# A two-layer hybrid backbone: filters from stacked fp32r features with mirrored slots side by side, and short convolutions made tile by tile with adding DMAs to DRAM

## The chip, the cores and the metric

The kernel runs on one core of one Trainium2 chip. The core has five engines with instruction streams of their own: TensorE (PE; its weight loads are listed as PEld), VectorE (DVE), ScalarE (ACT), GpSimd (POOL) and SyncE (SP), which here only issues DMAs. Sixteen DMA engines move data between DRAM, SBUF (128 partitions) and, through the compute engines, PSUM (8 banks per partition, where PE writes). The metric is device time in microseconds of one execution, the median of the runs.

## The reference

All is fp32 in and out: 2048 tokens of 1024 channels, 256 context tokens, two layers and a final norm. Layer 0 is a pooling mixer beside grouped-query attention (6 query heads, 2 key heads, 128 wide, 2304 keys). Layer 1 is a Hyena operator of order 2 on 768 channels beside a 2-D Fourier mixing on 256. What the change touches is in layer 1:

```python
def short_conv3(u, w, b):
    up = jnp.pad(u, ((0, 0), (1, 1), (0, 0)))
    return up[:, :-2] * w[0] + up[:, 1:-1] * w[1] + up[:, 2:] * w[2] + b

def hyena_filters(L, w1, b1, w2, b2, w3, freq):
    ...
    hdn = jnp.sin(fr * (hdn @ w2 + b2))
    h = (hdn @ w3).reshape(L, HY_ORDER, 2, HY_WIDTH)
    h = h * decay[:, None, None, :]
    h = h / (jnp.sum(jnp.abs(h), axis=(0, 2), keepdims=True) + EPS)
    zero = jnp.zeros((1, HY_ORDER, HY_WIDTH), f32)
    return jnp.concatenate([h[:, :, 0], zero, h[:0:-1, :, 1]], axis=0)

def hyena_mixer(u, ...):
    uc = short_conv3(u, conv_w, conv_b)
    v, x1, x2 = jnp.split(uc, HY_ORDER + 1, axis=-1)
    k = hyena_filters(L, w1, b1, w2, b2, w3, freq)
    z = v
    for o, gate_o in enumerate((x1, x2)):
        z = gate_o * (fft_long_conv(z, k[:, o]) + skip[o] * z)
    return z
```

So each of 3 x 768 channels gets a convolution with three taps over the tokens, and each of 768 channels two long convolutions with a filter of both directions, made from a small network of 64 hidden features.

## The kernel before

**Numbers.** Where accuracy needs it and speed allows it, a product is split: each operand into a high part of type fp32r and a low part, and three fp32r products are summed (`mm3`, L305, lines 306 to 308 of the profile). Small transforms run as plain fp32 products.

**Tokens.** Token 16 * n1 + n2 stands in slot n2 (16 of them, 128 tokens each), so that a row of 2048 tokens of one group of 128 channels is a tile of 128 channels x 16 slots x 128. The token before is the slot before, at the same n1; only for slots 0 and 15 it is slot 15 or 0, shifted by one n1.

**Stages, in order of time.** (1) Modulation, the filters' network (`hd2`, its hidden features, stored to DRAM in `hdd` in the order in which the groups will want them), layer 0's input projections. (2) Attention, by pairs of blocks of 128 queries. The order of its pieces is written out by hand in the strings of `BLOCK`: S scores, M and E the softmax, T transposes, V values, p a step of weight preparation (`weights`, L1371; ACT, POOL and SP), F or f a step of `filters` (L1116). (3) Layer 0's output projection, layer 1's norm, and layer 1's first four groups of columns (`FIRST`, `project0` at L1635); POOL meanwhile splits 25 tiles of weights, all of which stand ahead in its stream (L1733 to L1738). (4) The other 24 groups of columns, four at a time (`MGROUPS`, L482) over four blocks of 512 tokens, in 192 steps of 12 products (L1994), side by side with the long convolutions. (5) Fourier mixing and the first pass of the output projection. (6) Its last pass and the final norm.

**The order from stage 3 on** is made at build time by a planner (`Jobs`, L345). It keeps a clock; `pe(us)` lets it run on with each piece of PE's work; lanes (`Lane`) hand out the pieces of other work when the clock is within 2.5 us of their planned start; `at` puts a piece at a time; `store` queues a store on SP for the next step. An `Event` holds a lane until the planner has set its time. Each engine then runs its own stream in that order, and waits only for data and buffers.

**The filters (`filters`).** There are 12 units (6 groups of channels, 2 orders) of 8 groups of slots, in 18 steps each. A group takes slots a0 = 2 grp + 1 and a0 + 1 of the forward filter and their mirrored slots 16 - n of the backward one: it makes four products of the hidden features (64 x 128) with `w3` (L1173), multiplies by the decay (`ht`, L1174), makes a negated copy of the backward half (`hn`, L1175), sums absolute values for the norm (L1178, L1181), and adds the 128-point factor of the transform by eight products with the table `dft` (L1200, L1201), forward slot and mirrored slot into one sum. ACT copies to `Xs`, two halves of 64 channels (L1203). After the eighth group POOL runs the 16-point transforms (`fft16`) of the two halves, 6 operations per step, and SP stores the spectrum to `spec`.

**The short convolutions (`conv`, L1818).** In stages 3 and 4 `keep_cols` (L1517) copies a block's columns out of PSUM and stores them, as they are, to `ud` in DRAM. Each of 17 rows of channels is then read back whole (`cu`), and convolved in SBUF: ACT makes the middle term with the bias (`co`, L1829), the first tap in two halves (`tap`, L1834) and the last tap in place (L1842); five adding DMAs, issued from POOL, add the taps to `co`, shifted by a slot (L1837 to L1845). One row follows the other, with planned pauses `CV0` to `CV3` between the steps. The first row of all is convolved by ACT and DVE in `first_unit` (L1659).

**The long convolutions.** `s1` (L1853) turns a unit and makes the first factor, `conv_units` (L1944) runs both 16-point transforms and the product with the filter's spectrum on DVE, `s4` (L1885) makes the last factor on PE and gates with a short-convolved row on DVE. 12 units follow each other on DVE.

Of the kernel before, what the change touches and what calls it, by code (L numbers as in the profile page):

```python
# [20 lines left out]
P = 128  # L21
# [18 lines left out]
EARLY, LATE = (0, 1, 2, 6, 7), (3, 4, 5)  # L40

# [16 lines left out]
def constants():  # L58
    """Tables that depend on the shapes alone."""
# [30 lines left out]
    sel = [[2 * q + 1, (2 * q + 2) % 16, 15 - 2 * q, 14 - 2 * q] for q in range(8)]  # L90
    out["decay"] = np.stack([dec[:, :, q, :] for q in sel], 1)
# [36 lines left out]
def fft16(v, X, T, inv, s=None):  # L128
# [27 lines left out]
    def stt(out, in0, scalar, op, in1):  # L156
        """in0 already has its factor where s does the products, but for the sign"""
        if s is None and len(out.shape) > 3:
            for x in range(out.shape[1]):
                stt(out[:, x], in0[:, x], scalar, op, in1[:, x])  # L160
        elif s is None:
            put(out, lambda: v.scalar_tensor_tensor(out=out, in0=in0, scalar=scalar, in1=in1, op0=ALU.mult, op1=op))
        elif scalar > 0:
            tt(out, in0, op, in1)
        else:
            tt(out, in1, ALU.subtract, in0)
# [4 lines left out]
    tt(at(T, 0, *two), at(X, 0, *two), add, at(X, 2 * e, *two))  # L171
    tt(at(T, 2 * e, *two), at(X, 0, *two), sub, at(X, 2 * e, *two))
# [13 lines left out]
    def tan(n, *dims):  # L186
        """the slots from n on, times the tangent"""
# [16 lines left out]
    # the second four: slots k * e + b * o for b; 11 and 14 have the other sign  # L204
# [35 lines left out]
def tile_net(ctx, tc, i, k, out, keep=None):  # L240
# [9 lines left out]
    def mv(dst, src, eng=None):  # L250
        """a DMA of float32 words, of either type"""
# [22 lines left out]
    def y1_part(kk):  # L274
        """the place of gated channels of layer 1"""
# [6 lines left out]
    hdd = dram("hdd", (8, 64, 4, P))  # L282
# [30 lines left out]
    class Lane:  # L313
        """pieces for one engine, each of so many us, the next one at least so many later, or after an event"""
# [30 lines left out]
    class Jobs:  # L345
        """the order in which work is given to the engines: matrix products in front, the rest when they are that far"""
# [37 lines left out]
        def until(self, done):  # L384
            """let time pass until done()"""
# [15 lines left out]
    def load_wout(sp, wp, w, kks, dst, gb, wait=4.0, eng=sy, ve=v):  # L401
        """output projection times the gate, in two parts, one tile of rows at a time"""
# [21 lines left out]
    def load_gate(wp, n):  # L424
        """the gate of layer n, the same in every partition"""
# [4 lines left out]
    def rstd_steps(sp, ss, n, tag, scale):  # L430
        """ss [p, n] sums of squares -> 1 / sqrt(ss * scale + eps), with a Newton step after the square root"""
# [13 lines left out]
    def normed_steps(sp, xs):  # L445
        """each slab [p, D] of xs -> each row over its root mean square, in place"""
# [13 lines left out]
    def modulated_steps(sp, pp, xs, gs, sh, emit, lo_eng):  # L460
        """transposed, scaled and shifted, in two parts: emit(m) gives their places"""
# [1910 lines left out]
```

## Time and profile before

| what | us |
|---|---|
| median of 3 runs | 3173.34 |
| lowest and highest run | 3167.35, 3176.21 |
| span of the profiled execution, first to last instruction | 3162.6 |
| median less that span | 10.7 |
| PE busy | 2996.1 |
| DVE busy | 2183.2 |
| ACT busy | 1329.8 |
| POOL busy | 1215.5 |

The record gives one profiled execution, with its span and no separate time beside it; so sums are made against its span, and 10.7 us are added to compare with the median. Busy times overlap: an engine's share says how full it is over the whole span, and what sets the time in a stage has to be read in that stage. In the views, `out<-in` are the program's names, `128x512` partitions by elements, `[x <-ENGINE name]` the idle time of the engine before the instruction and what ended it. A plain fp32 product shows as two matmuls. "DMA share" is the mean busy share of the 16 DMA engines. SPq and POOLq are the streams in which SP and POOL issue DMAs.

### The profile page before, as it was taken

The page shows a single profiled execution, that of the slowest core. Times are in us where ns is not written, and L with a number is a line of the kernel's source. Part 1 is how long each engine was busy: PE and PEld are TensorE (multiplying, and loading weights), DVE is VectorE, ACT ScalarE, POOL GpSimd, SP SyncE. Part 2 cuts the span into 40 slices and gives each one's busy share as a digit, 9 for nine tenths or more (in the row PEclk, how much of TensorE's full clock was granted, in tenths as well). Part 3 has the DMA queues.
Part 4 walks back from the last instruction along what each step waited for, and adds up shares of the span by engine and source line. Part 5 has one row for each costly group of instructions (what it writes and reads, how often), then busy time and mean ns, then how long its engine had stood idle before and what let it go on. Part 6 is the DMA issues. An engine that isn't in the chain of part 4 may idle for free. (4 is left out here: it accounts for less than half of the span.)

```text
span 3162.6 us, 49927 instructions
## 1 busy us (share of the span) xinstructions
PE 2996.1 (95%) x18121; PEld 2589.2 (82%) x18121; DVE 2183.2 (69%) x4124; ACT 1329.8 (42%) x3130; POOL 1215.5 (38%) x1595
## 2 busy tenths in 40 slices
PE   8999999799999999999999999999989999988799
PEld 4888888699999998999898778777878787874587
DVE  4775437477777777777776443377789797978556
ACT  4444545355555555555556332322323232232123
POOL 3122223027888887878886344001010100101110
PEclk9999999899999999999999999999999999999899
DMA  6466345534444445444443777678899989976875
GB/s 223 157 202 202 125 132 162 182 107 127 121 140 132 128 127 169 121 125 133 117 115 117 250 261 256 242 258 283 275 290 288 293 282 314 275 260 167 233 210 176
DMA packets 425393, 614.72 MB, mean 194 GB/s; under 512 B 140278, under 2 KB 278200, under 8 KB 416698
## 3 DMA queue, kind: packets, MB, share of 16 engines
q1 hardware_dynamic: 399994, 528.43, 51.0%
q0 software_dynamic: 25152, 83.10, 11.2%
q8 instruction: 143, 2.34, 0.3%
q14 instruction: 104, 0.85, 0.1%
HBM read 388.60 MB, written 187.18 MB: 182 GB/s over the span
## 5 line engine op out<-in xcount | busy, mean ns | idle before, releaser
L303 DVE TENSOR_TENSOR pl<-pt,ph 128x512 fp32r<-128x512 f32 (+1 forms) x480 | 299.8, 633 | 137.1 <-ACT ph L300 136.1
L151 DVE TENSOR_TENSOR gB<-gB 128x256 f32<-128x256 f32 (+3 forms) x442 | 351.6, 845 | 51.2 <-ACT gB L1879 47.3
L300 ACT CAST ph<-pt 128x512 fp32r<-128x512 f32 (+1 forms) x480 | 253.5, 556 | 244.7 <-PE pt L1317 242.3
L306 PE MATMUL dacc<-dh,dw 128*128 128x512 f32 x768 | 312.2, 407 | 40.2 <-DMA dh<-h1T 39.5
L1306 ACT ACTIVATE pb<-S,mx 128x512 f32<-128x512 f32 (+1 forms) x480 | 309.7, 656 | 82.7 <-DVE mx L1298 59.4
L307 PE MATMUL dacc<-dh,dw 128*128 128x512 f32 x768 | 304.7, 397 | 0.0
L308 PE MATMUL dacc<-dh,dw 128*128 128x512 f32 x768 | 304.6, 397 | 0.0
L1295 DVE TENSOR_REDUCE mx<-S 128x1 f32<-128x512 f32 (+1 forms) x480 | 279.9, 629 | 18.6 <-DMA kh<-kT0h 14.0
L303 POOL TENSOR_TENSOR wl<-raw,wh 128x256 fp32r<-128x256 f32 x160 | 135.6, 880 | 368.6 <-ACT wh L300 356.7
L1317 PE MATMUL pt<-ident,pb 128*128 128x128 f32 x1728 | 248.0, 275 | 11.2 <-ACT pb L1306 10.9
L151 POOL TENSOR_TENSOR fX<-fT 128x128 f32<-128x128 f32 (+2 forms) x336 | 246.7, 757 | 4.9
L1329 PE MATMUL o<-ph,vh 128*128 128x256 f32 x864 | 233.0, 301 | 1.4 <-ACT ph L300 1.2
L151 POOL TENSOR_TENSOR fT<-fX 128x1024 f32<-128x1024 f32 (+1 forms) x192 | 202.6, 1081 | 49.0 <-ACT fX L1203 44.6
L1317 PEld LDWEIGHTS pt<-ident,pb 128*128 128x128 f32 x1728 | 197.2, 141 | 28.2 <-ACT pb L1306 14.8
L1330 PE MATMUL o<-ph,vl 128*128 128x256 f32 x864 | 216.5, 282 | 1.5 <-DMA vl<-vl 1.5
L306 PEld LDWEIGHTS dacc<-dh,dw 128*128 128x128 f32 x768 | 147.9, 193 | 78.2 <-DMA dh<-h1T 46.7
L306 PE MATMUL S<-kh,qh 128*128 128x512 f32 (+1 forms) x480 | 196.9, 410 | 9.9 <-DMA kl<-kT0l 8.2
L306 PE MATMUL acc<-wh,hh 128*128 128x256 f32 x672 | 197.2, 293 | 3.5 <-ACT qraw L969 2.4
L308 PE MATMUL acc<-wh,hl 128*128 128x256 f32 x672 | 193.1, 287 | 1.2 <-DVE hl L303 0.9
L307 PE MATMUL acc<-wl,hh 128*128 128x256 f32 x672 | 192.8, 287 | 0.9 <-POOL wl L303 0.8
L307 PE MATMUL S<-kl,qh 128*128 128x512 f32 (+1 forms) x480 | 180.4, 376 | 1.1 <-DMA kl<-kT0l 1.0
L308 PE MATMUL S<-kh,ql 128*128 128x512 f32 (+1 forms) x480 | 180.4, 376 | 0.0
(473 smaller groups left out, 7776.5 us busy)
## 6 DMA issues: line engine op xcount, KB each, us to landing
dh<-h1T SPq DMA_DIRECT2D x172, 512.0 KB
dec<-cst_decay_dram SPq DMA_DIRECT2D x96, 256.0 KB
spec<-fX SPq DMA_DIRECT2D x24, 1024.0 KB
dw<-wi SPq DMA_DIRECT2D x48, 512.0 KB
gK<-spec SPq DMA_DIRECT2D x48, 512.0 KB
raw<-in_ev_w_in_dram SPq DMA_DIRECT2D x160, 128.0 KB
u<-dev SPq DMA_DIRECT2D x70, 256.0 KB
cu<-u POOLq DMA_DIRECT2D x17, 1024.0 KB, 8.3
```

Source lines behind the costliest of these rows:

```text
L151: put(out, lambda: v.tensor_tensor(out=out, in0=in0, in1=in1, op=op))
L300: s.copy(hi, src)
L303: lo_eng.tensor_sub(lo, src, hi.bitcast(F32))
L306: pe.matmul(acc, ah, bh, start=first, stop=False)
L307: pe.matmul(acc, ah, bl, start=False, stop=False)
L308: pe.matmul(acc, al, bh, start=False, stop=last)
L1295: v.tensor_reduce(out=B["mx"][:, c : c + 1], in_=S[:, :n], axis=AX.X, op=ALU.max)
L1306: s.activation(B["pb"][:, c * 512 : c * 512 + n], B["S"][c][:, :n], AF.Exp, bias=B["mx"][:, 5:6], accum_out=B["sm"][:, c : c + 1])
L1317: pe.transpose(pt[:, t, :], B["pb"][:, (4 * c + t) * P : (4 * c + t + 1) * P], ident)
L1329: pe.matmul(gr["o"], vh[:, a, :], ph[:, t, :], start=a == 0, stop=False)
L1330: pe.matmul(gr["o"], vl[:, a, :], ph[:, t, :], start=False, stop=False)
```

## The change

**Filters.** The hidden features are split into a high and a low part and stacked to 128 rows; `w3` is split in the same way, each part held twice, one for each half of the rows. A group now takes a slot n and its mirror 16 - n (`PAIRS`; the last takes slots 0 and 8), both of the forward and of the backward filter: two slots, each with two products of K = 128, 256 wide, of type fp32r, the second slot's with forward and backward exchanged. The sign of the imaginary part stands in a new table `fdft`, and the transform's first step restores it (`conj`). So `hn` is gone, and the transform's factor takes four products of 256 columns, and in the last group four of 128 of a sum and a difference. The norm's sums are kept for the eight groups and reduced once. One transform of full width replaces two of half width, 4 operations per step instead of 6.

**Short convolutions.** They are made from each block of 512 tokens as it leaves PSUM, before anything is stored: ACT makes the middle term and the whole far tap of the block, DVE adds the other tap within the block and the piece kept from the block before, SP stores the sum to `ud`, and an adding DMA from POOL adds the far tap to `ud` in DRAM, shifted by a slot. The outermost slots of a row are kept (`edges`, `firstd`) and added at its end. `conv` only loads the finished row. The four `far` quarters lie where `cu` was. The three convolved rows of stage 3 are made in the same way in `first_conv`, straight from PSUM.

**Around these.** The last two groups of columns are ordered anew; `udone` is set 5 steps later; `hf` and the final gain take other buffers; `DE_` = 5 buffers for the blocks of columns. The planned delays are CV0 = 0.3, CV_S = 1.7, CV1 = 2.5, CV2 = 6 and CV3 = 10 us (before: CV0 to CV3 = 14, 12, 8, 15). In the diff, the products with `sd` are those of a unit's last group, and `jobs.until(lambda: not edges)` stands after the last step of stage 4.

```diff
-    MGROUPS = [..., (24, 25, 26, 27), (16, 22, 17, 23)]
+    MGROUPS = [..., (16, 22, 24, 25), (17, 23, 26, 27)]
...
+            s.copy(hd1.bitcast(F32R), hd2)
+            v.tensor_sub(hd2.bitcast(F32R), hd2, hd1)
+            for x, part in enumerate((hd1, hd2)):
+                for half in range(2):
+                    sy.dma_start(hdd[x * 64 : x * 64 + 64, 8 * half : 8 * half + 8, :],
+                                 part[half * 64 : half * 64 + 64].rearrange("p (a b) -> p a b", a=8))
...
-                    for q, n in enumerate((a0, a1, N2 - a0, (N2 - a1) % N2)):
-                        pe.matmul(acc[:, q, :], hd[:, q, :], w3[:, q // 2, :], start=True, stop=True)
-                    v.tensor_mul(ht, acc, dec)
-                    v.scalar_tensor_tensor(out=hn, in0=acc[:, 2:4, :], scalar=-1.0, in1=dec[:, 2:4, :], ...)
+                for q in range(2):
+                    for x in range(2):
+                        w = w3[:, x, ::-1] if q else w3[:, x]
+                        pe.matmul(acc[:, q], hd[:, q, :], w, start=x == 0, stop=x == 1)
+                v.tensor_mul(ht, acc, dec.unsqueeze(2).to_broadcast([P, 2, 2, P]))
...
-                            pe.matmul(fa[:, r, q, :], dft[:, n, r, :], ht[:, q, :], start=True, stop=False)
-                            pe.matmul(fa[:, r, q, :], dft[:, b, r, :], hn[:, q, :] if r else ht[:, 2 + q, :], ...)
+                            pe.matmul(fa[:, r, q], dft[:, b, r, :], sd[:, r, q], start=True, stop=True)
+                            pe.matmul(fa[:, r], dft[:, b, r, :], ht[:, q], start=q == 0, stop=q == 1)
+                s.copy(X[:, :, n : m + 1 : m - n, :], fa)
...
+    def short_conv(jobs, ep, mt, u, tb, up):
+        w0, w1, w2, o = taps(mt)
...
+        yield 0.0, CV0
+        mid = ep.tile([P, 4, P], F32, tag="ev", name="dm")
+        s.activation(mid, u, AF.Identity, bias=col2[:, PK2["cb"] + mt : PK2["cb"] + mt + 1], scale=w1)
+        far = nextfar()
+        s.mul(far, u, wf)
+        yield 0.0, CV_S
+        v.scalar_tensor_tensor(out=mid[:, own], in0=u[:, of], scalar=wn, in1=mid[:, own], op0=ALU.mult, op1=ALU.add)
+        if tb == first:
+            edges[mt] = ep.tile([P, P], F32, tag="eb", name="deb", bufs=4)
+        else:
+            v.tensor_add(mid[:, other], mid[:, other], edges[mt])
+        s.mul(edges[mt], u[:, next_], wn)
+        jobs.lanes[0].took(jobs.now, 0.8)
+        def put():
+            sy.dma_start(o[:, n0 : n0 + 4], mid)
...
+        def more():
...
+                add_to(o[:, n0 - 1 + x : n0 + 3], far[:, x:])
...
+        jobs.at(jobs.now + CV1, 0.0, put)
+        jobs.at(jobs.now + CV2, 0.0, more)
...
-            u = per.tile([P, N2, P], F32, tag="u", name="cu")
-            QU.dma_start(u, ud[mt].rearrange("p (a b) -> p a b", a=N2))
...
-            s.activation(o, u, AF.Identity, bias=..., scale=col2[:, 18 + mt : 19 + mt])
...
-                    g.dma_start(o[:, 1:9], t, accum_op=ALU.add)
...
-            g.dma_start(o[:, :15], u[:, 1:], accum_op=ALU.add)
-            g.dma_start(o[:, 15, : P - 1], u[:, 0, 1:], accum_op=ALU.add)
+            QU.dma_start(o, ud[mt].rearrange("p (a b) -> p a b", a=N2))
             yield 0.0, CV3
...
+            jobs.until(lambda: not edges)
```

More of the change, by code (lines that the diff above doesn't have):

```diff
@@ L40 @@
 EARLY, LATE = (0, 1, 2, 6, 7), (3, 4, 5)
+FIRST = (0, 1, 6, 7)
+PAIRS = [(n, N2 - n) for n in range(1, 8)] + [(0, 8)]
 BLOCK = [
@@ L89, in constants @@
     dec = dec.reshape(128, 16, NCH, P).transpose(2, 0, 1, 3)
-    sel = [[2 * q + 1, (2 * q + 2) % 16, 15 - 2 * q, 14 - 2 * q] for q in range(8)]
-    out["decay"] = np.stack([dec[:, :, q, :] for q in sel], 1)
+    out["decay"] = np.stack([dec[:, :, list(q), :] for q in PAIRS], 1)
+    fd = np.stack([dre, dim], 2)
+    fd[:, 9:, 1] *= -1
+    out["fdft"] = fd
     d = np.arange(256, dtype=f64)
@@ L170, in fft16 @@
     two = ((16, 2), (o, 4), (e, 2)) if inv else ((16, 2), (e, 2), (o, 4))
-    tt(at(T, 0, *two), at(X, 0, *two), add, at(X, 2 * e, *two))
-    tt(at(T, 2 * e, *two), at(X, 0, *two), sub, at(X, 2 * e, *two))
+    if conj:
+        for r, plus, minus in ((0, add, sub), (16, sub, add)):
+            for to, op in ((0, plus), (8, minus)):
+                tt(at(T, r + to, (1, 8)), at(X, r, (1, 8)), op, at(X, r + 8, (1, 8)))
+    else:
+        tt(at(T, 0, *two), at(X, 0, *two), add, at(X, 2 * e, *two))
+        tt(at(T, 2 * e, *two), at(X, 0, *two), sub, at(X, 2 * e, *two))
     row = (o, 4)
@@ L281, in tile_net @@
     wevd, wod = ([dram(f"w{x}{kk}", (P, 2, D)) for kk in range(KD)] for x in "eo")
-    hdd = dram("hdd", (8, 64, 4, P))
+    firstd = [dram(f"first{mt}", (P, P)) for mt in range(18)]
+    hdd = dram("hdd", (P, N2, P))
     fnd = dram("fn", (P, 2, 2, 256))
@@ L1654, in project0, with first_conv, rest, edge @@
                 jobs.pe(0.65 * len(ns))
+        before = {}
+        def first_conv(n, mt, u, tb):
+            w0, w1, w2, o = taps(mt)
+            n0 = 4 * tb
+            mid = ep.tile([P, 4, P], F32, tag="ev", name="cm")
+            s.activation(mid, u, AF.Identity, bias=col2[:, PK2["cb"] + mt : PK2["cb"] + mt + 1], scale=w1)
+            low = ep.tile([P, P], F32, tag="cl", name="cl", bufs=3)
+            s.mul(low, u[:, 0], w2)
+            def rest():
+                for to, of, w in ((slice(1, 4), slice(0, 3), w0), (slice(0, 3), slice(1, 4), w2)):
+                    v.scalar_tensor_tensor(out=mid[:, to], in0=u[:, of], scalar=w, in1=mid[:, to], op0=ALU.mult, op1=ALU.add)
+                if tb:
+                    v.tensor_add(mid[:, 0], mid[:, 0], before[n])
+                else:
+                    before[n] = ep.tile([P, P], F32, tag=f"cb{n}", name="cb", bufs=1)
+                s.mul(before[n], u[:, 3], w0)
+                dve.took(jobs.now, 1.4)
+                jobs.store(o[:, n0 : n0 + 4], mid)
+                if tb == 0:
+                    jobs.store(firstd[mt], low)
+                jobs.at(jobs.now + 4.0, 0.0, edge)
+            def edge():
+                if tb:
+                    add_to(o[:, n0 - 1], low)
+                if tb == NB - 1:
+                    add_to(o[:, 0, 1:], before[n][:, : P - 1])
+                    add_to(o[:, 15, : P - 1], firstd[mt][:, 1:])
+            jobs.at(jobs.now + 1.3, 0.0, rest)
         columns = [Event() for _ in range(NB)]
@@ L1991, in tile_net @@
         with ExitStack() as ps:
-            ep = pool(ps, "d_e", DE)
+            ep = pool(ps, "d_e", DE_)
+            u8 = per.tile([P, N2, P], F32, tag="u", name="far")
+            convlane.append(jobs.lane())
+            fars.extend(u8[:, 4 * x : 4 * x + 4] for x in range(4))
             pm = pool(ps, "d_ps", 1, PSUM)
```

202 lines of the change are left out of this document (106 added, 96 removed).

## The prediction

> **What bounds the kernel now.** I first read the windows view with the span cut at the kernel's stages: layer 0's projections to 655 us, attention with the filters woven in to 1744, layer 0's output projection and layer 1's first columns to 2075, layer 1's remaining columns beside the long convolutions to 2802, Fourier mixing and the first output pass to 3055.5, the last pass. Columns: length, then busy us and instructions of PE, PEld, DVE, ACT, POOL, then granted clock, DMA share, GB/s.
>
> ```profile
> 0.00:655.00 655.00, 605.45 (x3781) 524.21 (x3782) 372.54 (x762) 299.42 (x792) 155.48 (x195) 0.97 0.53 170
> 655.00:1744.00 1089.00, 1070.89 (x7854) 981.68 (x7852) 828.75 (x1693) 619.93 (x1681) 851.11 (x1141) 1.00 0.45 128
> 1744.00:2075.00 331.00, 318.02 (x1536) 262.67 (x1536) 135.66 (x218) 100.98 (x196) 101.31 (x126) 0.98 0.68 243
> 2075.00:2802.00 727.00, 685.65 (x3568) 582.27 (x3569) 602.06 (x994) 205.80 (x262) 68.93 (x86) 0.97 0.91 289
> 2802.00:3055.50 253.50, 216.96 (x960) 158.59 (x958) 178.67 (x304) 64.69 (x109) 38.05 (x46) 0.92 0.80 218
> 3055.50:3162.60 107.10, 99.09 (x426) 79.80 (x426) 65.53 (x157) 38.97 (x95) 0.57 (x2) 0.98 0.50 164
> ```
>
> PE is the longest engine in every stage. In attention it is busy 1070.9 of 1089 us at clock 1.00, while POOL (78%) and DVE (76%) have room: what is taken from PE there shortens the stage. In the column stage PE lacks 41 us, DVE is at 83% and the DMA engines at 91%. Second, the waits view, PE's largest wait in attention and in the column stage (total us, times, longest):
>
> ```profile
> PE pt L1317 <- ACT pb L1306: 7.5, 10, 0.8
> ...
> PE dacc L306 <- DMA dh<-h1T: 39.5, 18, 8.3
> ```
>
> Attention has almost no stall; the column stage's stall is one thing, the layer's input arriving late.
>
> **Attention: the filters' products.** There are 12 units of 8 groups. A group now makes 4 products with K = 64 (`hacc`) and 8 with the transform's table (`fa`), all fp32 and 128 wide; each shows as two matmuls, and the source view counts 96 groups of 8:
>
> ```profile
> L1173 PE MATMUL hacc<-w,hd x768: 271/272/579, 611.5 to 1636.5; 64*128 64x128 f32 x192
> ```
>
> The timeline gives slots from start to start (start us, duration, engine, line):
>
> ```profile
> 900.87 1.16 PE L1173 MATMUL hacc<-w,hd 64*128 64x128 f32 x8
> 901.96 0.39 PE L1329 MATMUL o<-ph,vh 128*128 128x256 f32 x1
> 902.18 0.28 PE L1330 MATMUL o<-ph,vl 128*128 128x256 f32 x1
> 902.29 0.28 PE L1329 MATMUL o<-ph,vh 128*128 128x256 f32 x1
> ...
> 905.36 0.38 PE L1200 MATMUL fa<-ht,fdft 128*128 128x128 f32 x2
> ...
> 907.14 0.27 PE L1317 MATMUL pt<-ident,pb 128*128 128x128 f32 x1
> ...
> 2828.38 12.25 PE L2100 MATMUL hacc<-M,G 128*128 128x256 f32 x56
> ```
>
> `hacc` takes 901.96 - 900.87 = 1.09 us, `fa` 907.14 - 905.36 = 1.78 us, together 2.87. A 256-wide fp32r product, as in attention's values, follows its neighbour after 0.115 to 0.12 us; a 256-wide fp32 product is two of the last row's matmuls, 2 x 12.25/56 = 0.44 us (0.43 without the pipeline's tail).
>
> After the change `hacc` is 4 fp32r products 256 wide: 4 x 0.12 = 0.48 us. The first fp32r product after fp32 ones costs 0.22 rather than 0.12 (901.96 to 902.18), and the K = 64 slot has 1.09 - 8 x 0.111 = 0.20 us beyond its matmuls. Such switches may stay (0.48 + 0.20) or vanish (0.48, and 0.10 less after it); I take 0.58, a saving of 0.51, ends 0.41 and 0.71. `fa` is 4 fp32 products 256 wide, 1.73, saving 0.05; in a unit's last group it is 4 of 128, 0.89, saving 0.89. Per unit 8 x 0.51 + 7 x 0.05 + 0.89 = 5.3 us; 12 units: **64 us**, ends 54 and 83.
>
> Does the stage follow? The reciprocal-row multiplies at L1348 come once per pair of query blocks; six pairs with filters, and one without:
>
> ```profile
> 650.29 0.42 DVE L1348 TENSOR_TENSOR rb<-prb,bsg 128x256 f32<-128x256 f32 x1 [1.72 <-PE prb L1346]
> ...
> 794.90 0.42 DVE L1348 TENSOR_TENSOR rb<-prb,bsg 128x256 f32<-128x256 f32 x1 [2.02 <-PE prb L1346]
> ...
> 1718.71 0.42 DVE L1348 TENSOR_TENSOR rb<-prb,bsg 128x256 f32<-128x256 f32 x1 [1.11 <-PE prb L1346]
> 1737.82 0.42 DVE L1348 TENSOR_TENSOR rb<-prb,bsg 128x256 f32<-128x256 f32 x1 [1.22 <-PE prb L1346]
> ```
>
> A pair takes (794.90 - 650.29)/6 = 24.1 us with filters, 19.1 without. Taking 64/43 = 1.5 us off ((1636.5 - 611.5)/24.1, some 43 pairs, hold filters) gives 22.6, well above that floor. I take 62 of the 64.
>
> The rest of the filter edit lies beside PE. DVE loses `hn` and the running sum in each group, and gains in each unit a 1024-element reduction, two 256-element sums and the split of `w3`:
>
> ```profile
> L1178 DVE TENSOR_REDUCE rd<-ht 128x128 f32<-128x512 f32 x88 | 94.1, 1069 | 0.0
> L1181 DVE TENSOR_TENSOR rd<-rd 128x128 f32<-128x128 f32 x77 | 38.6, 502 | 2.6
> L1175 DVE SCALAR_TENSOR_TENSOR hn<-hacc,dec 128x256 f32<-128x256 f32 x88 | 36.5, 415 | 0.0
> ```
>
> Minus 8 x 0.415 + 7 x 0.50, plus 2 x 1.07 + 3 x 0.42: 3.4 us less per unit. ACT has one 512-wide copy for two 256-wide ones, SP the same two loads per group at half the bytes. POOL's two half-width transforms become one of double width: the same elements in half the instructions, so POOL, 78% busy, gets no more to do. At the start, one ACT copy and one DVE subtraction of 1024 elements (about 1.1 and 1.3 us) split the network's output, and 4 stores replace 10 on SP; nothing waits for them before 611 us, so zero (if the cover were gone, 2.4 us).
>
> **First columns (1744 to 2075).** Twelve tiles get, beside the copy that becomes the middle term, two 128-wide ACT multiplies and two DVE taps, and their banks are held until DVE has read them. PE is 96% busy on its own work, so most hides; the last tile's taps stand before the next stage's first use of that bank: about 1.3 us planned plus two taps of 0.56, so **+3 us**, ends 0 and 10. The adds stand on POOL behind its 25 weight splits, which end just after the second block's evictions:
>
> ```profile
> 1980.66 0.59 POOL L252 DMA_DIRECT2D wi<-iw  x1 [0.30 <-POOL iw L1737]
> ...
> 1956.26 1.95 ACT L1522 COPY dev<-cacc 128x512 f32<-128x512 f32 x3 [17.58 <-PE cacc L308]
> ```
>
> The second block's `low` tiles wait some 20 us for POOL; the third block, which reuses them, comes a quarter of this stage's 331 us later, so nothing stops.
>
> **Column stage.** Moved in: 14 rows of columns in 4 tiles, 56 tiles, each with two 512-wide and one 128-wide ACT operation, a DVE tap of 384, for three tiles in four a DVE sum of 128, a 256 KB store on SP, and a 256 KB adding DMA on POOL. Removed: per row one whole-row load, four ACT passes, and 2 MB of adding DMAs into SBUF; one plain load of 1 MB stays. Prices, with DVE's waits:
>
> ```profile
> L162 DVE SCALAR_TENSOR_TENSOR gB<-gB 128x256 f32<-128x256 f32 x136 | 50.2, 420 | 0.9
> L162 DVE SCALAR_TENSOR_TENSOR gB<-gB 128x128 f32<-128x128 f32 x68 | 16.6, 285 | 0.0
> ...
> DVE co L1913 <- PE go L1904: 51.6, 13, 6.9
> DVE gB L151 <- ACT gB L1879: 47.3, 5, 19.1
> ```
>
> DVE: 384 elements extrapolate to 0.420 + 0.135 = 0.56 us; 56 x 0.56 + 42 x 0.285 = **43 us more**. Against it stand the 47.3 us in which DVE waited for a unit's first factor: the first of them fall while convolutions 1 and 6 were passing through their serial chain of loads and adds, and with finished rows in DRAM that chain is one load. I count 35 of them as gone, the gaps before these two transforms early in the stage (start, duration, what, and the idle time before in brackets).
>
> ```profile
> 2143.48 10.49 DVE L151 TENSOR_TENSOR gB<-gB 128x2048 f32<-128x2048 f32 x8 [19.09 <-ACT gB L1879]
> ...
> 2235.90 10.49 DVE L151 TENSOR_TENSOR gB<-gB 128x2048 f32<-128x2048 f32 x8 [16.37 <-ACT gB L1879]
> ```
>
> So DVE ends some 8 us later by itself, with the 51.6 us of waits for PE as slack, and PE's gain can show.
>
> DMA, by queue in this stage, then by queue in 2940 to 3060, where 30 adds into DRAM of 256 KB make up the software queue, and their time to landing:
>
> ```profile
> q1 hardware_dynamic: 56960, 162.55, 62.0%
> q0 software_dynamic: 12384, 46.65, 28.6%
> ...
> q0 software_dynamic: 4316, 7.86, 41.4%
> ...
> DMA to landing us min/median/max: 3.5/5.9/10.1
> ```
>
> Plain transfers run at 162.55/(0.62 x 727) = 0.36 MB/us of all engines. The software queue's 208 us hold some 16.8 MB of plain loads (47 us), so its adds cost 161. An add into DRAM costs 0.414 x 120/30 = 1.66 us; 56 make 93. That is 68 us less, and the share falls from 0.91 to about 0.82. The 39.5 us of late input came where the engines were full; I take 23 back, ends 0 and 39.5. At the end the plan lets time pass until the last edge is added, 0.3 + 1.7 + 6 = 8 us by the diff's delays, in which DVE gets transform work ahead of the Fourier fold: +8, ends 0 and 8. The stage and its successor together: -23 + 8 = **-15 us**.
>
> **Sum.** -62 + 3 - 15 = -74. The profiled execution's span is 3162.6 us; the median of the runs, 3173.3, lies 10.7 above it. 3088.6 + 10.7 = **3099 us**.
>
> **Rivals.**
> *Everything shows* (0.13): no switch cost, all input stalls gone, and some of the 37 us that PE lacks from 2802 to 3055: -83 + 3 - 42 = -122, 3051 us. For it: PE is the bound everywhere. Against: the stage after 2802 is paced also by DVE's last units.
> *POOL or SP paces the filters* (0.13): the transform is issued 4 double operations at a time over 11 of a unit's 18 steps, so it comes in bursts, with the weight splits between; a late POOL makes SP's weight stores wait, and the filter loads stand behind these on SP. If this eats 42 of 62: -32, 3141. Against it: POOL's 78%.
> *DVE paces the columns* (0.16): the 43 us aren't repaid, since DVE also loses the slack that PE's stalls gave it (51.6 us of waits for PE); the last convolution ends later and PE waits for it. -62 + 3 + 28 = -31, 3142; if the full 43 stands, 3157.
> *The quarter buffers block ACT, slower than before* (0.11): the four `far` quarters rotate over three tiles per block of 727/24 = 30 us, so one is wanted again about 32 us after it was filled; its add is issued 1.7 + 6 = 7.7 us after that, may wait on POOL behind row loads, and lands after 3.5 to 10.1 us. Past some 14 us of delay ACT stands in its multiply, the accumulators behind it aren't emptied, and PE stops. At 7 us a block, the 16 blocks of three tiles cost 112: -62 + 3 + 112 = +53, 3226. It decides from 59/16 = 3.7 us a block. The store on SP is tighter: it is planned 2.5 us after the DVE tap, and a tap that DVE does later than that holds the input loads queued behind it on SP. Against: POOL's issues are short under a busy DVE, as this row from the column stage shows (ns, min/median/max).
>
> ```profile
> L1837 POOL DMA_DIRECT2D co<-tap x17: 839/842/891, 2076.4 to 2899.5; - x17
> ```
>
> [...]
> That fp32r at 256 doesn't run in one pass I hold at nothing, since attention's values run so at 0.12 us.
>
> **How the numbers follow.** The forecast has 0.47. Below 3045 lies about half of the first rival, above 3165 the fourth and a little of the third: 0.2 in all. Range 3045 to 3165; the forecast's own, by the ends of its terms, 3065 to 3130. About 0.3% (9.5 us) can be told from no change. Faster: 0.47 + 0.13 + 0.12 + 0.13 = 0.85; the same 0.05, from the second, third and fourth; slower 0.10, the fourth.
>
> **What would show it.** Right: attention's pairs at 22 to 23 us; `hacc` slots near 0.5 to 0.7; the wait of `dacc` for `dh` under 20 us; DMA share near 0.82; DVE in the column stage near 92%. Wrong: pairs still at 24 with PE waiting for `hacc`'s inputs; ACT standing in the `far` multiply; DVE's last inverse transform ending later relative to PE's first pass. The forecast falls if attention shortens by less than 30 us.

## The result, and the profile after

The changed kernel takes **3211.7 us** (median of 4 runs, 3209.0 to 3212.2); the kernel before took 3173.35 beside it. The ratio is 1.012, with a 95% interval of 1.0107 to 1.0132: slower by 38 us, where 74 less were forecast. The profiled executions' spans are 3209.8 and 3162.6 us, 47.2 apart. An execution of the changed kernel takes 1.8 us more than its span (3211.6 and 3209.8), so by the same difference the profiled execution of before took some 3164 us, less than its timed runs, and about 9 of the 47 us come from this.

The windows view of the changed kernel, cut at the same places as before (length, then busy us and instructions of PE, PEld, DVE, ACT, POOL, granted clock, DMA share, GB/s):

```profile
0.00:656.00 656.00, 603.78 (x3729) 521.62 (x3730) 370.91 (x756) 300.51 (x790) 156.38 (x195) 0.96 0.53 169
656.00:1740.00 1084.00, 1009.40 (x6754) 911.73 (x6752) 788.70 (x1554) 615.85 (x1600) 766.60 (x637) 0.98 0.37 122
1740.00:2086.50 346.50, 316.24 (x1536) 261.57 (x1536) 162.73 (x280) 107.65 (x219) 114.90 (x140) 0.97 0.65 226
2086.50:2830.00 743.50, 692.45 (x3536) 586.27 (x3537) 593.98 (x1002) 213.42 (x370) 79.62 (x97) 0.96 0.83 260
2830.00:3103.00 273.00, 221.67 (x974) 164.26 (x973) 215.15 (x368) 53.16 (x108) 29.31 (x36) 0.89 0.66 189
3103.00:3209.80 106.80, 99.20 (x445) 80.59 (x443) 66.62 (x156) 37.08 (x88) 0.00 (x0) 0.98 0.50 171
```

Read it stage by stage against the rows of before. Attention (second row): PE's busy time fell by 61.5 us, 1070.9 to 1009.4, as forecast; but the stage fell by 5, since PE's idle time rose from 18 to 75. The first columns grew from 331 to 346.5, the column stage from 727 to 743.5 although its DMA share fell to 0.83, the Fourier stage from 253.5 to 273. So four things went wrong, one in each of four stages.

**Attention.** First the sizes of the edit. The timeline of the changed kernel gives the new slots, from start to start:

```profile
702.93 1.89 PE L1225 MATMUL fa<-ht,fdft 128*128 128x256 f32 x8
704.47 0.47 PE L1351 MATMUL o<-ph,vh 128*128 128x256 f32 x1
...
707.96 0.64 PE L1193 MATMUL hacc<-w3s,hd 128*128 128x256 f32 x4
708.44 0.82 PE L1339 MATMUL pt<-ident,pb 128*128 128x128 f32 x6
```

`hacc` takes 0.48 us (forecast 0.58, lower end 0.48), `fa` 1.54 (forecast 1.73). The pairs begin at 22.5 us (674.10 - 651.59), the pace that was forecast, but some take over 30:

```profile
651.59 0.42 DVE L1370 TENSOR_TENSOR rb<-prb,bsg 128x256 f32<-128x256 f32 x1 [1.98 <-PE prb L1368]
674.10 0.42 DVE L1370 TENSOR_TENSOR rb<-prb,bsg 128x256 f32<-128x256 f32 x1 [1.11 <-PE prb L1368]
...
1400.42 0.42 DVE L1370 TENSOR_TENSOR rb<-prb,bsg 128x256 f32<-128x256 f32 x1 [1.90 <-PE prb L1368]
1433.20 0.42 DVE L1370 TENSOR_TENSOR rb<-prb,bsg 128x256 f32<-128x256 f32 x1 [1.97 <-PE prb L1368]
```

What happens in the pair of 32.8 us (1400.42 to 1433.20) is in the timelines of POOL, ACT and PE:

```profile
1388.08 4.77 POOL L156 TENSOR_TENSOR fT<-fX 128x1024 f32<-128x1024 f32 x2
1392.92 9.40 POOL L156 TENSOR_TENSOR fX<-fT 128x1024 f32<-128x1024 f32 x4
1402.40 2.52 POOL L156 TENSOR_TENSOR fT<-fX 128x512 f32<-128x512 f32 x2
...
1410.19 1.26 POOL L1425 TENSOR_TENSOR wraw<-wraw,wgb 128x512 f32<-128x512 f32 x1
1411.48 0.62 ACT L1403 CAST wodd<-wraw 128x512 fp32r<-128x512 f32 x1 [8.83 <-POOL wraw L1425]
1412.62 1.12 PE L1339 MATMUL pt<-ident,pb 128*128 128x128 f32 x4 [7.57 <-ACT pb L1328]
```

POOL works without a pause at the filter's transform from 1388 to 1410. The multiply of the output weights with the gate (L1425) stands behind it; ACT's cast of the product (L1403) waits 8.83 us for it; behind the cast stand ACT's exponentials (L1328), and PE's transposes wait 7.57 us for these. Over attention, in the waits view (ACT of before, then ACT and PE of the changed kernel):

```profile
ACT wodd L1381 <- POOL wraw L1403: 6.2, 4, 2.3
```

```profile
ACT wodd L1403 <- POOL wraw L1425: 67.0, 13, 12.1
...
PE pt L1339 <- ACT pb L1328: 25.9, 33, 7.6
PE hacc L1193 <- ACT fX L1226: 12.4, 6, 7.1
...
PE smacc L1206 <- DVE rs L1203: 6.3, 6, 1.9
PE fa L1223 <- DVE sd L1216: 5.9, 4, 2.7
```

**End of the first columns.** PE's last product of `cacc` starts at 2071.6; the next stage's first begins at 2086.8:

```profile
2061.17 0.78 ACT L1749 ACTIVATE cm<-cacc,col 128x512 f32<-128x512 f32 x1 [0.80 <-PE cacc L319]
...
2073.41 0.37 ACT L1760 ACTIVATE cb<-cacc,col 128x128 f32<-128x128 f32 x1 [11.20 <-DVE cm L1757]
...
2086.37 0.37 ACT L1760 ACTIVATE cb<-cacc,col 128x128 f32<-128x128 f32 x1 [5.92 <-DVE cm L1757]
...
2086.83 0.76 PE L317 MATMUL dacc<-dh,dw 128*128 128x512 f32 x1 [14.82 <-ACT cb L1760]
```

The three tiles go one after the other through ACT, DVE and ACT again. DVE's taps lie between its operations of the first unit's transform (up to 4.6 us at a time), so from `cm` to `cb` the three tiles hold their banks for 12, 5.5 and 7 us, and PE stands 14.8 us.

**Column stage.** In the waits view, DVE, SP's queue and PE:

```profile
DVE dm L1578 <- ACT dm L1574: 114.9, 49, 9.9
SPq L1587 <- DVE dm L1582: 67.5, 37, 4.0
PE dacc L317 <- DMA dh<-h1T: 37.9, 15, 6.1
```

One block in the timelines (DVE's taps, then ACT's middle terms):

```profile
2200.64 1.22 DVE L2066 TENSOR_TENSOR gB<-gB,gK 128x1024 f32<-128x1024 f32 x1
2207.28 0.62 DVE L1578 SCALAR_TENSOR_TENSOR dm<-dev,col,dm 128x384 f32<-128x384 f32 x1 [5.43 <-ACT dm L1574]
2210.56 0.62 DVE L1578 SCALAR_TENSOR_TENSOR dm<-dev,col,dm 128x384 f32<-128x384 f32 x1 [2.46 <-ACT dm L1574]
2212.56 0.62 DVE L1578 SCALAR_TENSOR_TENSOR dm<-dev,col,dm 128x384 f32<-128x384 f32 x1 [1.17 <-ACT dm L1574]
...
2206.45 0.80 ACT L1574 ACTIVATE dm<-dev,col 128x512 f32<-128x512 f32 x1
2209.72 0.81 ACT L1574 ACTIVATE dm<-dev,col 128x512 f32<-128x512 f32 x1 [1.18 <-DMA sg<-dev]
2211.73 0.80 ACT L1574 ACTIVATE dm<-dev,col 128x512 f32<-128x512 f32 x1
```

DVE is empty-handed from 2201.9 to 2213.3 but for 2.7 us of taps, since each tap stands in its stream before the work of the long convolutions, and ACT has copied four banks before it makes the first middle term. SP's store (L1587) waits for the tap, with the input loads `dh` behind it; PE waits 37.9 us for these, hardly less than before (39.5). DVE's taps by themselves cost what was forecast (55 at 0.618 us and 41 at 0.285, from the groups view, against 56 at 0.56 and 42 at 0.285).

**Fourier stage.** PE now waits for DVE, which is late with the last units:

```profile
PE go L2005 <- DVE gB L156: 10.6, 1, 10.6
...
PE gt__28655 L1966 <- DVE co L2014: 8.4, 1, 8.4
```

### The profile page after: what moved, and what is told of

It is laid out like the page before. It is cut to its first block, busy times and chain, and to the rows that moved or that the text cites. A ratio compares the mean times of both kernels' runs of the same rounds, so it can differ in the third digit from the quotient of the medians.

```text
span 3209.8 us, 47168 instructions
## 1 busy us (share of the span) xinstructions
PE 2942.7 (92%) x16969; PEld 2526.0 (79%) x16969; DVE 2198.1 (68%) x4112; ACT 1327.7 (41%) x3171; POOL 1146.8 (36%) x1105
## 5 line engine op out<-in xcount | busy, mean ns | idle before, releaser
L317 PE MATMUL dacc<-dh,dw 128*128 128x512 f32 x768 | 313.2, 408 | 52.9 <-DMA dh<-h1T 37.9
L1328 ACT ACTIVATE pb<-S,mx 128x512 f32<-128x512 f32 (+1 forms) x480 | 309.1, 654 | 92.6 <-DVE mx L1320 57.2
L1339 PE MATMUL pt<-ident,pb 128*128 128x128 f32 x1728 | 253.6, 276 | 34.1 <-ACT pb L1328 32.8
L1546 POOL DMA_DIRECT2D u<-far x56 | 52.7, 984 | 597.6 <-DMA u<-dm 457.7
L156 POOL TENSOR_TENSOR fX<-fT 128x256 f32<-128x256 f32 (+2 forms) x168 | 218.9, 1326 | 2.0
L156 POOL TENSOR_TENSOR fT<-fX 128x1024 f32<-128x1024 f32 (+2 forms) x120 | 190.6, 1618 | 56.0 <-ACT fX L1226 54.3
L1554 ACT COPY dev<-dacc 128x512 f32<-128x512 f32 x56 | 33.0, 588 | 360.5 <-PE dacc L319 269.5
```

The costliest lines, as they stand in the source:

```text
L156: put(out, lambda: v.tensor_tensor(out=out, in0=in0, in1=in1, op=op))
L317: pe.matmul(acc, ah, bh, start=first, stop=False)
L1328: s.activation(B["pb"][:, c * 512 : c * 512 + n], B["S"][c][:, :n], AF.Exp, bias=B["mx"][:, 5:6], accum_out=B["sm"][:, c : c + 1])
L1339: pe.transpose(pt[:, t, :], B["pb"][:, (4 * c + t) * P : (4 * c + t + 1) * P], ident)
```

## The experiments

Medians are in us; "saved" is against the changed kernel's 3211.7, and ratios are to the kernel before on the same chip. In the diffs, `...` marks what is left out, and constants that stand in one long line of the kernel are shown by themselves.

**Each half alone**, put on the kernel before: first the filters with the old short convolutions, then the short convolutions with the old filters.

```diff
-                        pe.matmul(acc[:, q, :], hd[:, q, :], w3[:, q // 2, :], start=True, stop=True)
+                        pe.matmul(acc[:, q], hd[:, q, :], w, start=x == 0, stop=x == 1)
...
-                    ops += [fn for fn, _ in fft16(g, Xs[x], T, False, g)]
+                    ops += [fn for fn, _ in fft16(g, X, T, False, g, True)]
```

```diff
-            s.copy(ev, acc)
-            jobs.store((ud[mt] if mt < 18 else fid[mt - 24])[:, bl], ev)
+            s.copy(ev, acc)
+            convlane[0].add(short_conv(jobs, ep, mt, ev.rearrange("p (a b) -> p a b", a=4), tb, up))
...
-            s.activation(o, u, AF.Identity, bias=..., scale=col2[:, 18 + mt : 19 + mt])
+            QU.dma_start(o, ud[mt].rearrange("p (a b) -> p a b", a=N2))
```

> The filters' half of the change alone, the short convolutions as before. In the changed kernel PE lost 61.5 us of busy time in attention (1070.9 to 1009.4) but the stage shrank by only 5, as PE's idle time rose from 18 to 75. Theory: GpSimd's transforms in batches of four double-width operations (9.4 us for four of 1024 elements) delay the weight products that stand behind them, ScalarE stands behind those (67 us of waits against 6), and PE's transposes behind ScalarE; this lies in attention alone, so the filters alone give 3173 - 5 = 3168 us, no measurable change. Rival: the short convolutions' stages cost more because of the filters' half (another end of attention, other buffers), so part of the later 51 us stays here: 3180 to 3210.

> The short convolutions' half alone, the filters as before. Theory: all of the loss behind attention (+15 first columns, +16 column stage, +20 Fourier stage, 51 us in all) belongs to this half: 3173 + 51 = 3224 us. The prediction's working for this half, fewer DMA bytes and no serial chain, would give 3173 + 3 - 15 = 3161. Rival: it is shared between the halves: 3190 to 3210.

The filters alone: 3169.75, ratio 0.9993 (0.9981 to 1.0006), no change. The short convolutions alone: 3207.6, ratio 1.011 (1.0093 to 1.0127), 37 us more than before, not 51, which lies in the range of the rival (3190 to 3210, the loss is shared). By the stretches of the table further down, the second half alone loses 33.8 us behind attention (12.4 in the first columns, 4.4 in the column stage, 17.0 after it), the first half alone 7.8, and the two together 50.3. So most of the loss belongs to the second half, and the first half has no gain to set against it; some 9 us come only with both, and why isn't shown.

**GpSimd's transform, by size.** Operations are issued by the time that the kernel estimates for each (1.15 us for one of 128x1024, for which GpSimd took 2.39 in the changed kernel's trace), 2.2 us a step, which is two large ones.

```diff
-            for op in ops[:n]:
+            us = 0.0
+            while ops and us < n:
+                op, t = ops.pop(0)
+                us += t
...
-            del ops[:n]
```

> The changed kernel, but GpSimd gets the transform's operations by their size (about 4.5 us of work per step, two of the 1024-wide ones) and no longer four at a time (up to 9.4 us). Same operations, same order. Theory: ScalarE's waits for GpSimd's weight products (67 us) fall below 25, PE's idle time in attention from 75 to about 30, and the time by some 40 us: 3170. Rival: attention's loss is in the new end of each unit on VectorE (1024-wide reduction, the sum and difference; ScalarE waits 33 us for the norm there): no change, 3211.

3203.5, ratio 1.0103 (1.008 to 1.0126): 8 us saved where 40 were expected, and ACT still waited 66.9 us for the products. So the size of a batch was not the cause. In the next run, called the spread transform below, the same is issued thinner (n = 1.8), and the store of the spectrum is due 1 step after the last operation in place of 4:

> The changed kernel with GpSimd's transform metered as in the run with two large operations per step, but thinner (about 3.7 us per step), so that it fills nearly all 16 steps of a unit in which operations are issued, as six operations a step did before (94 in 16 steps), and with its store due 1 step later, not 4. In the run with 4.5 us per step ScalarE still waited 66.9 us for the weight products, so the size of a batch was not it. Theory now: the whole transform in 12 or 13 of 16 steps asks 4.6 us of GpSimd per step beside the weights, in steps of some 4.4 us, so a backlog grows in each unit and the weight products stand behind it; spread thinner, the wait falls below 25 us and the time by some 35: 3175. Rival: what GpSimd waits for (72 us for loads of weights that SyncE issues late, behind weight stores that wait for GpSimd) is the cause; then the wait stays near 67 and the time near 3203.

3177.8, ratio 1.0029 (1.0015 to 1.0043): 34 us saved. The windows view of attention, from the first pair's multiply (L1348, now L1370) to the last's, of before, of the changed kernel, and of this run:

```profile
650.30:1769.40 1119.10, 1098.95 (x8062) 1007.11 (x8060) 848.07 (x1732) 638.98 (x1729) 860.09 (x1152) 1.00 0.45 130
```

```profile
651.60:1766.30 1114.70, 1036.64 (x6958) 936.50 (x6956) 808.29 (x1593) 635.21 (x1648) 774.90 (x648) 0.98 0.37 121
```

```profile
650.30:1731.50 1081.20, 1029.34 (x6958) 932.00 (x6956) 810.93 (x1594) 636.72 (x1648) 777.44 (x649) 0.99 0.39 125
```

In the waits view, SP's wait at the spectrum's store in the changed kernel, then ACT's wait for the products and SP's at that store in this run:

```profile
SPq L1142 <- POOL fX L156: 6.1, 2, 6.0
```

```profile
ACT wodd L1405 <- POOL wraw L1427: 28.7, 11, 7.6
...
SPq L1144 <- POOL fX L156: 95.4, 12, 19.8
```

With the same work on POOL (777 us against 775), ACT's wait falls from 67 to 28.7 and the stage by 33.5. The theory puts this down to the rate: a unit's transform has 46 operations (552 in POOL's groups, 12 units), so four a step finish it in 12 of the unit's 16 steps and let it queue up, where six a step of twice as many, of half the size, had filled all 16. That the rate did it isn't shown. By the kernel's own estimates this run takes 13 steps, not 16, and in the trace the ninth unit's transform, from its first operation to its last, lies on POOL as long as in the changed kernel: from 1366.3 to 1428.5 us here, from 1383.4 to 1444.3 there. The other edit did change something: SP now stands 95.4 us at the spectrum's stores, and its later loads and stores wait behind them. Which of the two edits gave the 34 us stays open. The rival's cause, weights that are loaded late, hasn't gone: POOL waits 75.4 us for them here and 65.0 in the changed kernel.

**The product on another engine.**

```diff
-                        g.tensor_mul(raw, raw, gb)
+                        v.tensor_mul(raw, raw, gb)
```

> The changed kernel, with the 32 products of the output weights with the gate done by VectorE in place of GpSimd (same operation). This takes the step in which ScalarE waits for GpSimd out of GpSimd's queue, and 41 us of work off GpSimd. Theory: ScalarE's 67 us of waits for it fall below 15, PE's idle time in attention from 75 to below 40, the time to about 3175. Rival: the loads of these weights are late, so ScalarE waits as long for the same products, and VectorE now stands behind them too: 3211 or more.

3193.05, ratio 1.0072 (1.0055 to 1.0088): 19 us saved, half of what was expected, and ACT waits 31.8 us for the product on DVE instead. Both theories hold in part: POOL's queue was the larger share of the wait, and the engine that takes the product passes on its own queue.

**The filters alone, with the transform spread.**

> The filters' half alone, with GpSimd's transform spread thinly over the unit's steps as in the run that spread it. With batches of four this half was level with the kernel before (3169.8). Theory: what the spread gave the whole change in attention (33 us) it gives here too: 3170 - 33 = 3137 us, which is then the filters' half without its side effect, a little over half of the 62 us that was forecast. Rival: without the later stages' other disorder the gain is taken back behind attention (the column stage is paced by its input and DMA): 3155 to 3170.

3135.6, ratio 0.9892 (0.9875 to 0.9908): 37 us less than before beside it, as expected. This is the filters' half with less of its side effect: ACT still waits 30.3 us for the products.

**Banks copied out at the end of the first columns.**

```diff
+            if tb == NB - 1:
+                kept = ep.tile([P, 4, P], F32, tag="ev", name="ku")
+                s.copy(kept, u)
+                u = kept
...
-    DE = 4
+    DE = 5
```

> The changed kernel, but in the last block of the first columns ScalarE copies the three banks to SBUF first, and the taps read the copies (a fifth buffer for this). Theory: PE's 14.8 us of standing before the column stage, with the slower matmuls right after it, goes: 3211 - 15 = 3196. Rival: VectorE, which does these taps between the operations of the first unit's transform, is as late afterwards, and PE waits for it later instead: 3211.

3200.1, ratio 1.0086 (1.007 to 1.0102): 12 us saved. PE's wait there is 8.1 us in place of 14.8, and no longer for the taps; what it waits for now the profile doesn't show.

**Taps and stores in the column stage.** The pause before the tap, `CV_S`, from 1.7 to 4.5; in a run by itself the delays of the store and the add, `CV1` and `CV2`, from 2.5 and 6 to 6 and 10; then the later tap with the store right behind it.

```diff
-    CV1, CV2, CV_S = 2.5, 6, 1.7
+    CV1, CV2, CV_S = 2.5, 6, 4.5
```

```diff
-    CV1, CV2, CV_S = 2.5, 6, 1.7
+    CV1, CV2, CV_S = 6, 10, 1.7
```

```diff
-    CV1, CV2, CV_S = 2.5, 6, 1.7
+    CV1, CV2, CV_S = 0.3, 6, 4.5
```

> The changed kernel with the pause between ScalarE's middle term and VectorE's tap at 4.5 us in place of 1.7 (the planner issues up to 2.5 us ahead, so 1.7 puts the tap into VectorE's stream at once). VectorE stood 115 us at these taps. Theory: this standing makes VectorE the pace of the long convolutions and of the Fourier stage behind them; it falls below 40 us, and the time by 25 to 35: 3180. Rival: the taps' 43 us of work itself is the cost, or PE's waits for input: 3205 to 3211.

> The changed kernel with each tile's store 6 us after its tap in place of 2.5, its adding DMA 10 us in place of 6. SyncE stood 74 us at these stores with the input loads behind them, and PE still waits 38 us for input though the DMA share fell from 0.91 to 0.83. Theory of late issue: PE's wait for input falls below 20 us, time 3211 - 15 = 3196. Rival: the input is late for another reason (the reuse of its buffers, the queue's own pace), PE's wait stays near 38 and the time at 3211.

> As the run with the taps later (pause 4.5 us, 3145.7 us), but with each tile's store issued 0.3 us after its tap in place of 2.5. It tells apart what that run relieved: VectorE's standing at the taps, or SyncE's standing at the stores with the input loads behind them. If VectorE's standing was the cost, the time stays near 3146, the column stage near 678 us. If SyncE's was, SyncE stands at the stores again (23 us there to 70 or more), PE's wait for input goes from 6 back towards 38 us, the column stage towards 715 us, the time to 3180.

The later tap: 3145.7, ratio 0.9918 (0.9904 to 0.9933): 66 us saved, twice what was expected; DVE's standing at the taps fell from 114.9 to 46.7 us, PE's wait for input from 37.9 to 6.3. The later store: 3182.3, ratio 1.0037 (1.0023 to 1.0051): 29 saved, also twice what was expected, with 13.3 us of waits for input. The later tap with an early store: 3135.9, ratio 0.9895 (0.9872 to 0.9918), an interval that overlaps the one of the later tap alone. The column stage in these three, in this order:

```profile
2090.60:2768.70 678.10, 669.62 (x3538) 571.90 (x3539) 596.96 (x1010) 212.86 (x369) 79.31 (x97) 0.99 0.90 285
```

```profile
2087.60:2802.40 714.80, 681.82 (x3538) 581.27 (x3539) 595.34 (x1004) 213.37 (x369) 80.00 (x97) 0.97 0.87 270
```

```profile
2079.30:2759.70 680.40, 671.11 (x3554) 574.79 (x3555) 602.22 (x1024) 212.62 (x369) 79.54 (x97) 0.99 0.90 287
```

In the waits view of the last of them, SP's queue and PE:

```profile
PE dacc L317 <- DMA dh<-h1T: 7.3, 5, 3.0
...
SPq L1587 <- DVE dm L1582: 19.5, 13, 5.3
```

With the store right behind a later tap, SP stands 19.5 us at it and not 67.5, and PE's wait for input stays at 7.3. Since SP's standing didn't come back, this run doesn't price it apart from DVE's. What the three show is one chain, tap too early in DVE's stream, store, input loads, PE; it can be opened at either link, and best at the first. DVE's work in the stage is the same in all (594 to 602 us); it was the standing, not the work, that cost.

**The mends together.** The spread transform, the copied banks and the later tap; then with the product on DVE, and stores and adds at 4 and 8 us.

> The changed kernel with the three mends together: the transform spread (34 us by itself), the last block's banks copied (12), the pause before the tap at 4.5 us (66). If the three losses are separate, as the theory has it, they add: 3211.7 - 34 - 12 - 66 = 3100 us, which is where the prediction stood (3099). If VectorE or another engine paces all of it in the end, less comes back: 3115 to 3135.

> As the three mends together, and the output weights' product on VectorE, each store 4 us and each adding DMA 8 us after its tap. Theory: ScalarE's remaining 29 us of waits for the weight products shrink and SyncE's last 23 us at the stores go: 5 to 15 us less than the three mends. Rival: the wait for the product only moves to VectorE (32 us there when it was tried), and nothing is gained over the three.

The three: 3102.5, ratio 0.9784 (0.9769 to 0.9798): 109 us saved; 34 + 12 + 66 = 112 were expected. So the three gains add up, and the losses are separate within the noise. The four: 3098.8, ratio 0.9769 (0.9752 to 0.9786), not to be told from the three. Both beat both kernels.

**What stays behind the columns.** With the three mends, the stretch from the last column step to the end is still 374.0 us against 360.2 before. In it the load for the second Fourier fold stands 14.3 us on SP for the edges' adding DMA, whose memory it takes over. The next run puts both convolved groups of columns into the last group of steps but one; the run after it has the product on DVE and CV1 = 0.3 as well:

```diff
-    MGROUPS = [..., (16, 22, 24, 25), (17, 23, 26, 27)]
+    MGROUPS = [..., (16, 17, 24, 25), (22, 23, 26, 27)]
```

> As the run with three mends (3102.5), with the last eight columns grouped so that both short-convolved ones (16, 17) are in the last but one group and the last group has none: the same work, but no tap, store, adding DMA or edge stands at the end of the columns. Theory of the end chain: the load for the second Fourier fold, which in that run stands 14.3 us on SyncE behind the edges' adding DMA (VectorE 9.3 and PE 7.7 us behind it), comes at once, and the stretch behind the columns falls from 374 to about 362 us: 3090. Theory of VectorE's work: the work is the same and only earlier by a block, the stretch stays within 3 us of 374: 3100.

> As the run before it in this list, with the output weights' product on VectorE and each store directly behind its tap (0.3 us). Expected if the mends go on adding: about 3 us for the product (3102.5 to 3098.8 with it) and up to 10 us for the early store (3145.7 to 3135.9 with it): 3078 to 3088. Rival: nothing beyond the run before it, 3090.

3106.7, ratio 0.9796 (0.9773 to 0.9818), and 3108.8, ratio 0.9798 (0.9775 to 0.9821): no gain over the three mends. The load no longer stands for the edges, and the stretch is 376.6 us, not 362. PE waits for DVE's last transform in its place (waits view, three mends, then columns regrouped):

```profile
PE go L2011 <- DVE gB L156: 7.8, 1, 7.8
...
SPq L2179 <- DMA u<-deb: 14.3, 1, 14.3
```

```profile
PE go L2011 <- DVE gB L156: 17.2, 1, 17.2
```

The stretch itself in the windows view of the regrouped columns:

```profile
2733.30:3109.90 376.60, 317.58 (x1416) 239.97 (x1415) 275.63 (x512) 88.49 (x192) 26.84 (x33) 0.92 0.62 185
```

So the theory of the end chain falls: taken away, it gives nothing. DVE is busy 275.6 us in this stretch, against 243.8 before, and that fits the other theory, that the taps' work pushes DVE's last units into it. That DVE's work alone is the cause wasn't tried by taking it away; it is what is left, not shown.

## Why the prediction was wrong

The table gives the change of each stretch of the profiled span against before (cut at the first and last pair of attention and at the first and last column step), for the changed kernel and for the one with three mends.

| stretch | forecast | changed kernel | three mends |
|---|---|---|---|
| up to attention's first pair | 0 | +1.3 | +0.6 |
| attention | -62 | -4.4 | -34.7 |
| first columns | +3 | +14.8 | +6.6 |
| column stage | -15, with the next | +16.1 | -52.4 |
| Fourier, output | | +19.4 | +13.8 |
| sum | -74 | +47.2 | -66.1 |

**PE's saving: right, in part by luck.** PE was 62.3 us less busy in attention (1098.95 to 1036.64). The switch costs vanished, and `fa` gained more than was taken: by the slots shown a group saves 0.61 us in `hacc` and 0.24 in `fa`, not 0.51 and 0.05, which makes 89 us in the prediction's sum (82 with 1.71 for the old `fa`, the median of its 96 slots). The granted clock in this stretch was 0.98 in place of 1.00, which by an estimate lengthens 1037 us of busy time by some 20 (1037 x 0.02); that this is the difference isn't shown.

**"I take 62 of the 64": wrong, the largest miss.** The step compared the new pair time with the floor of 19.1 us without filters, which says nothing of POOL. That "POOL, 78% busy, gets no more to do" was right for the total (POOL's busy time fell) and missed the order in which it comes: while they last, the elements are issued at four thirds of the old rate, and a product that another engine needs stands behind them. The rival "POOL or SP paces the filters" names this with a chance of 0.13 and 42 of the 62 us. 58 were eaten, by another way than it names: SP's wait for POOL's part of the weights did rise (134 to 260 us), but no load behind it is among PE's waits. ACT waited 67 us for one product, and PE's own waits rose by 33 us for ACT and by 22 for DVE. Of the latter, 12 us (6.3 + 5.9, and 2.8 before) are for the new end of a unit on DVE, which the prediction costed as DVE's time alone. That the product in POOL's queue costs time is shown by the run that takes it out (attention 18.5 us shorter). With the spread transform PE is still idle for 51.9 us there (1081.20 - 1029.34), 20.2 before; what the rest waits for wasn't tried apart. A reading beside it, "the same two loads per group at half the bytes", is wrong too: `hd` has as many bytes as before and only the decay has half; nothing hung on it.

**First columns, +3 (0 to 10): mis-sized.** It took the planned 1.3 us and two taps. The taps of three tiles follow each other through ACT and DVE, and DVE was in the first unit's transform: PE stood 14.8 us, and by an estimate some 2.4 us went into slower matmuls after it (12 products 0.43 us apart in place of 0.23).

**DMA relief: right in sign, its size and its reason not.** The share fell to 0.83 (forecast 0.82), but over a longer stage: 0.83 x 743.5 = 617 us of all engines against 0.91 x 727 = 662, so 45 less where 68 were forecast. The 39.5 us of late input stayed (37.9), since it had a new cause. With the taps later it fell to 6.3, 33 less than before, where 23 were taken; but the share was 0.90 in that run, hardly below the 0.91 of before. So it isn't shown that the input came late because the engines were full, and what relieved it stays open.

**DVE in the columns: the work right, the standing missed.** 43 us of taps were forecast, and the taps' rows give 0.618 x 55 + 0.285 x 41 = 46. Against them the slack of DVE's old waits was set; but the taps brought 115 us of new waits, because each stands right behind the ACT operation that feeds it. All of DVE's waits in the stage came to 118 us before and to 143 now; its work there fell from 602 to 594 us in spite of the taps, and behind the columns it rose from 244 to 282. The planned pause of 1.7 us is less than the 2.5 us by which the planner issues ahead, so in DVE's stream there was no pause at all. The text of the slow rival has the second link, "a tap that DVE does later than that holds the input loads queued behind it on SP", but as something that might happen past some delay. The rival that came true in the columns is "DVE paces the columns" (0.16), in its outcome; its reason, the work of the taps, is not what cost.

**End of steps, +8:** a wait was there (10.7 us on SP in the changed kernel; 14.3 on SP and 9.3 on DVE with three mends), but removing it gave nothing.

**The far buffers:** the mechanism of the slow rival did not decide; no wait of ACT's `far` multiply stands in the waits view of the stage. The adds landed after 2.7, 8.2 and 17.5 us (min, median, max).

**The chances:** the rivals were priced as if one at a time could come true. Two of them came true together, with the forecast's +3 exceeded: -62 + 58 + 15 + 16 + 19, and +1 ahead of attention, is the +47 measured. As they lie in different stages they should have been added: by the prediction's own prices, 42 and 43 us on top of -74 are +11, on the slow side. The forecast's number, 3099, is nearly what the kernel takes with three mends (3102.5), but by other terms, attention half as much, the columns more than twice; that the two agree is luck.

## What to carry to other kernels

When an edit makes an engine's work come in a new rhythm, compare its rate in the stretch where it runs with what that engine has free there, and name every instruction of another engine that waits in the same queue; a share of busy time over the stage doesn't show it (here POOL's fell from 78% to 71% in attention, while ACT's wait for its product rose from 6.2 to 67.0 us). An operation that is fed by another engine cost its wait as well as its length where no other work stood between the two in both streams (46 us of taps brought 115 us of waits with a planned pause of 1.7 us, and 46.7 with 4.5), so give a planner a pause larger than the distance by which it runs ahead, here 2.5 us. Rivals in different stages are no alternatives: add their prices. And look in the trace whether a run did what its name says: the spread transform lay on its engine as long as the one that it replaced, and the run had a second edit.

## What the runs showed of the hardware

PE's stop of 14.8 us at the end of the first columns cost more than its length. The windows view of the changed kernel around it (length, PE busy, clock, DMA share, GB/s):

```profile
2071.00:2086.80 15.80, 1.01 (x5) 0.63 0.50 147
2086.80:2092.10 5.30, 5.27 (x13) 0.50 0.99 344
2092.10:2099.00 6.90, 6.90 (x32) 0.99 0.97 239
```

After the stop the granted clock is 0.50 for 5.3 us, and products start 0.43 us apart in place of 0.23; in the next 6.9 us it is 0.99. In the column stage the same matmuls took 692.6 us of PE's busy time at clock 0.96, with 15 waits for input (37.9 us), and 669.6 at 0.99 with the tap later and 6 such waits (6.3 us): 23 of that run's 65 us in this stage. What sets the granted clock these rows don't show.

POOL's issues of the 56 adds from `far` took 841, 860 and 2733 ns (min, median, max). The row that the prediction shows has 891 at most, but other adds of before took up to 1197. What made some of them longer isn't shown. The longer ones decided nothing: ahead of all the adds of this kind POOL waited 457.7 us for the stores to land.
